# The second conformer block in the memory of the first, and the late delta-rule groups in the first priority class

## The chip, the cores and the metric

The kernel runs on one core of a Trainium2 chip. The metric is device time in microseconds (us), the median of several runs. The engines are TensorE (PE in the profile; PEld is its weight load), VectorE (DVE), ScalarE (ACT), GpSimd (POOL) and SyncE (SP, whose work here is a queue of DMA transfers). Each engine takes its own instructions strictly in the order in which the program lists them.

## The reference

One layer of a hybrid trunk over 2048 prompt tokens and 32 sample tokens, width 1024. All mixers read one normalised input; their outputs stand side by side in front of one output projection:

```python
h = rmsnorm(x, norm_mix)
z = h @ w_in                              # one projection for all three mixers
a = gated_deltanet(z, state_gdn)          # 4 heads x 128, short conv, delta rule
s = s5(z, state_s5)                       # 16 x 16 channels, complex diagonal scan
c = swish(layernorm(causal_dwconv31(glu(z), state_conv)))   # conformer, 256 wide
x = x + concat([a, s, c]) @ w_out
u = rmsnorm(x, norm_ffn)
x = x + (silu(u @ w1) * (u @ w3)) @ w2    # hidden 2816 = 22 tiles of 128
x = x + sigmoid(x @ pe_gate) * (p @ pe_w)
y = rmsnorm(x, norm_final)
```

The depthwise convolution of the conformer has 31 taps over time. The delta rule goes through the tokens in order, with a state that is handed on, so the group of tokens b waits for the group of tokens b-1.

## The kernel before, in words

The tokens are cut into four blocks of 512; the last one also carries the 32 sample tokens (544 columns, worked as 2 x 272). Activations lie transposed, features on the partitions. Every matrix product of the trunk is made in three passes of eight matmuls (high half by high half, high by low, low by high: names ending in `h` and `l`, as `fah`, `fal`, `wh_w`, `wl_w`), all at line 122 in `dense`. The low halves of the weights are made at L98, on VectorE or POOL.

The program runs in two phases. Phase A projects blocks 0 to 3 (A0 to A3; weights `wh_qkv`, `wh_z`). Phase F does the rest, block by block (F0 to F3): the output projection (`wh_out`, its operand split into `fah` and `fal` at L1134 and L1136 from tiles `hb` that a DMA brings from `mixT`, L1155), the residual (L1173), the norm (sums of squares L1167, then L154, L68 to L70), the hidden tiles j = 0 to 21, each a product with w1 (evacuated by L1196, L1199) and one with w3 (L1201, L1202, the split L1204). They go in groups of four with two tiles ahead, and then follows the product with w2 (L1218). After that come eight gate tiles (`wh_gate`, evacuated by L1242 into `gth`, L1243 into `hb`), the final norm (L1253 on VectorE) and the store (L1254). The results of the dense products share three PSUM buffers (`ps_d`).

The mixers ("heads") run beside these products. Each is a Python generator; a chain of generators is advanced one step whenever a certain number of matmul columns has been emitted (7168, in F0 9216), and each `yield` ends a step. What the steps write is:

- `conformer_block`: 31 taps for each of two halves of the channels (L824 opens, L826 sixty times, on VectorE, from `xc` and `cacc` in SBUF), then transposes (`ps_ct` L837, `ps_cf` L856), the layer norm, and the result to `mixT` (L865).
- `gdn_group`: one delta-rule group of 256 tokens, two per block, and one for the 32 sample tokens after block 3. Preparation (L909 to L947), a triangular inversion by many small steps (L982, L983), a trip through memory and `XT` (L992), the state part (`ps_vn` L1069, `ps_s` L1076, `ps_o` L1083 and L1084, on VectorE L1060, L1071, L1079), a norm (L1093 to L1101), transposes `ps_ot` (L1109), `zy` (L1110) and the DMA to `mixT` (L1111).
- the S5 units.

Block 0's mixers run during A1 to A3. After phase A, `later_heads` is one chain: conformers 1 and 2, delta rule 1, S5, delta rule 2, conformer 3, delta rule 3 with the sample group. Before each F block the chain is run until that block's mixers are complete.

The order on each engine is made when the program is built: a scheduler plays the program through on a model, and takes among the instructions that are ready the one with the lowest priority number. There are three classes, `first` (evacuations, loads, what an F block does outside its products), `heads` and `later` (the dense products and whatever the chain of heads emits). Within a class the order is that of emission. `at(which)` selects the class for what is emitted inside it. Memory also sets the order: a tile that reuses another's memory waits for that tile's last reader.

Of the kernel before, what the change touches and what calls it, by code (L numbers as in the profile page):

```python
# [1257 lines left out]
def trunk_kernel(ctx: ExitStack, tc: tile.TileContext, A):  # L1258
# [7 lines left out]
    @contextmanager  # L1266
    def at(which):
        old = getattr(G, "cur", None)
        if old is not None:
            G.pr[old] = tc.cur_priority  # L1270
        G.cur = which
        tc.cur_priority = G.pr[which]
        yield
        G.pr[which] = tc.cur_priority
        G.cur = old
        if old is not None:
            tc.cur_priority = G.pr[old]
# [33 lines left out]
    NB = G.NB  # L1311
# [60 lines left out]
    R = lambda name, bufs=1: tc.tile_pool(name=name, bufs=bufs, side="right", reuse_waits="tile")  # L1372

    def conf(b, wp):
        return conformer_block(G, A, b, wp, G.psM)

    def gdn_part(b, i, S, sp):
        S = yield from gdn_group(G, A, sp, G.psM, G.tp_, b * 4 + 2 * i, P, 2, S, b, 256 * i)
        if b == NB - 1 and i == 1:
            nc.sync.dma_start(A.gdn_p, S)  # L1380
            Sd = G.kp.tile([P, NH, P], F32, tag="S", name="Sd0")
            nc.sync.dma_start(Sd, A.st_gdn)
            Sd = yield from gdn_group(G, A, sp, G.psM, G.td_, 0, TS, 1, Sd, b, BLK)
            nc.sync.dma_start(A.gdn_s, Sd)
        return S

    state = [S]

    def conf_of(b):
        with R(f"cc_{b}") as wp:  # L1390
            yield from conf(b, wp)

    def s5_of(u):
        with R(f"s5_{u}") as wp:
            yield from s5_unit(G, A, u, wp, G.psM)

    def gdn_of(b):
        with R(f"gd_{b}", 2) as sp:
            for i in range(2):
                state[0] = yield from gdn_part(b, i, state[0], sp)  # L1400

    def run(*gens):

# [3 lines left out]
    with ExitStack() as cx:  # L1407
        pa = PhaseA(G, A, cx)
        pa.block(0)

        box = {}

        def first_s5():
            while "w5" not in box:
                yield 1
            yield from s5_unit(G, A, 0, box["w5"], G.psM)
            box["done"] = True

        def first_heads():
            with R("s5i") as tp:  # L1420
                yield from s5_init(G, A, tp, G.psM)
            with R("s5_0") as w5:
                box["w5"] = w5
                yield from conf_of(0)
                yield from gdn_of(0)
                while "done" not in box:
                    yield 1

        G.start(first_heads())
        for b in range(1, NB):  # L1430
            if b == G.UB:
                G.start(first_s5())
            pa.block(b)
        if NB == G.UB:
            G.start(first_s5())
        G.flush()
# [2 lines left out]

    def later_heads():  # L1440

        first = list(range(1, min(3, NB)))
        with ExitStack() as cx2:
            wps = [cx2.enter_context(R(f"cc_{b}")) for b in first]
            for b, wp in zip(first, wps):
                yield from conf(b, wp)
        for b in range(1, NB):
            if b not in first:
                yield from conf_of(b)
            if b % G.UB == 0:  # L1450
                yield from s5_of(b // G.UB)
            yield from gdn_of(b)
            ready[0] = b

    G.start(later_heads())
    for b in range(NB):
        G.flush(lambda: ready[0] >= b)
# [117 lines left out]
```

## Time and profile before

| | us |
|---|---|
| median of 3 runs | 2885.08 |
| lowest, highest | 2883.63, 2887.02 |
| profiled execution | 2883.21 |
| its span in the trace | 2881.4 |
| TensorE busy | 2760.5 (96%) |
| VectorE busy | 1737.5 (60%) |
| mean granted TensorE clock | 0.977 |

The page cuts the span in 40 equal slices of 72 us and gives the busy share of each engine in tenths. A row of the timeline has the start, the duration, the engine, the line, the operation with output and inputs, the count of equal operations merged in it, and in brackets the idle time ahead of it with what ended it. A row of a group has the count, the busy time and the mean in ns, then the idle time ahead.

A3 ends at 667.8 us in the trace, F1's first product is at 1228.2, F2's at 1776.3 and F3's at 2342.7.

### The profile page before, as it was taken

What the parts mean: (1) busy time and instruction counts of PE and PEld (TensorE: products, weight loads), DVE (VectorE), ACT (ScalarE), POOL (GpSimd) and SP (SyncE); (2) the same over time, 40 slices, a digit from 0 to 9 for tenths busy, and PEclk for the clock granted to TensorE, in tenths of its full rate; (3) what the DMA queues carried; (4) which work ended last, traced back from release to release, by engine and by line L of the source; (5) the groups of instructions that cost most, each with busy time, mean ns of one, the idle gap of its engine ahead of it and who ended that gap; (6) DMA issues with size and microseconds to landing.
All of it is one profiled execution on the core that took longest, in us unless ns stands there. A gap on an engine that the chain in (4) does not pass through costs nothing.

```text
span 2881.4 us, 41027 instructions
## 1 busy us (share of the span) xinstructions
PE 2760.5 (96%) x15300; PEld 2363.4 (82%) x15300; DVE 1737.5 (60%) x3933; ACT 937.7 (33%) x1409; POOL 560.0 (19%) x460
## 2 busy tenths in 40 slices
PE   7899989997999999999999999999999979999997
PEld 5668778896888888888888887788888769999997
DVE  8969765896647575665664646864663733333343
ACT  4243422323322222433423333342332423222232
POOL 4732321243333242421000101100010110000000
PEclk9999999998999999999999999999999979999998
DMA  6588776674555564686665657566565564555553
GB/s 225 169 265 262 252 229 220 202 224 166 195 184 191 167 198 162 221 270 214 213 192 171 191 165 247 190 207 193 171 195 151 193 206 155 176 175 176 176 184 105
DMA packets 278919, 565.32 MB, mean 196 GB/s; under 512 B 67344, under 2 KB 126880, under 8 KB 278576
## 3 DMA queue, kind: packets, MB, share of 16 engines
q1 hardware_dynamic: 278720, 562.70, 60.7%
q8 instruction: 121, 1.98, 0.3%
q14 instruction: 78, 0.64, 0.1%
HBM read 457.76 MB, written 104.25 MB: 195 GB/s over the span
## 4 chain that ended last, share of the span: by engine, by line
PE 78%; DVE 11%; DMA 5%; issue 2%; ACT 2%; SPq 1%; POOL 0%; DVEq 0%; ACTq 0%; POOLq 0%
PE ps_d L122 70%; DVE cacc L826 1%; PE ps_kk L935 1%; DVE gacc L625 1%; DMA sild<-gacc 1%; PE ps_q L1013 1%; PE ps_z L1026 1%; PE ps_o L1084 1%; PE ps_o L1083 1%; PE ps_s L1076 1%; DVE ct L982 0%; PE ps_ks L1056 0%; DVE cx L983 0%; PE ps_vn L1069 0%; DVE hb L1253 0%
## 5 line engine op out<-in xcount | busy, mean ns | idle before, releaser
L94 ACT ACTIVATE wh_w<-wr_w 128x1024 fp32r<-128x1024 f32 (+1 forms) x272 | 281.4, 1035 | 759.6 <-PE ps_d L122 553.5
L122 PE MATMUL ps_d<-fah,wh_w 128*128 128x512 f32 (+1 forms) x1760 | 376.8, 354 | 6.1 <-DVE hb L1173 3.5
L122 PE MATMUL ps_d<-fah,wl_w 128*128 128x512 f32 (+1 forms) x1760 | 376.5, 353 | 0.0
L122 PE MATMUL ps_d<-fal,wh_w 128*128 128x512 f32 (+1 forms) x1760 | 372.7, 352 | 0.0
L122 PEld LDWEIGHTS ps_d<-fah,wh_w 128*128 128x128 f32 x1760 | 291.2, 189 | 52.1 <-issue 4.5
L122 PEld LDWEIGHTS ps_d<-fal,wh_w 128*128 128x128 f32 x1760 | 291.3, 188 | 43.9
L122 PEld LDWEIGHTS ps_d<-fah,wl_w 128*128 128x128 f32 x1760 | 290.9, 189 | 43.1
L1218 DVE TENSOR_TENSOR hb<-hb,ps_d 128x512 f32<-128x512 f32 (+1 forms) x240 | 140.0, 585 | 192.5 <-PE ps_d L122 192.0
L122 PE MATMUL ps_d<-acth,wh_w 128*128 128x512 f32 (+1 forms) x880 | 210.4, 354 | 0.0
L122 PE MATMUL ps_d<-acth,wl_w 128*128 128x512 f32 (+1 forms) x880 | 209.9, 353 | 0.0
L122 PE MATMUL ps_d<-actl,wh_w 128*128 128x512 f32 (+1 forms) x880 | 208.7, 353 | 0.0
L826 DVE SCALAR_TENSOR_TENSOR cacc<-xc,cc_w,cacc 128x512 f32<-128x512 f32 (+1 forms) x240 | 177.9, 775 | 0.0
L122 PEld LDWEIGHTS ps_d<-actl,wh_w 128*128 128x128 f32 x880 | 149.0, 188 | 22.4
L122 PEld LDWEIGHTS ps_d<-acth,wh_w 128*128 128x128 f32 x880 | 148.2, 188 | 22.5 <-issue 0.2
L122 PEld LDWEIGHTS ps_d<-acth,wl_w 128*128 128x128 f32 x880 | 148.5, 188 | 21.8
L98 POOL TENSOR_TENSOR wl_w<-wr_w,wh_w 128x1024 fp32r<-128x1024 f32 (+1 forms) x46 | 107.6, 2339 | 254.0 <-ACT wh_w L94 228.1
L1196 DVE TENSOR_TENSOR fa<-ps_d,bc 128x512 f32<-128x512 f32 (+1 forms) x110 | 64.7, 589 | 141.2 <-PE ps_d L122 134.1
L1201 DVE SCALAR_TENSOR_TENSOR fth<-ps_d,bc 128x512 f32<-128x512 f32 (+1 forms) x110 | 64.8, 589 | 129.1 <-PE ps_d L122 128.5
L122 PE MATMUL ps_d<-hh,wh_qkv 128*128 128x512 f32 (+1 forms) x480 | 105.6, 363 | 17.0 <-DVE raw L615 15.2
L1204 DVE TENSOR_TENSOR actl<-fa,acth 128x512 fp32r<-128x512 f32 (+1 forms) x110 | 87.7, 797 | 44.3 <-ACT acth L1203 43.9
L122 PEld LDWEIGHTS ps_d<-hh,wh_qkv 128*128 128x128 f32 x480 | 81.4, 194 | 31.5 <-issue 17.0
L122 PE MATMUL ps_d<-hh,wl_qkv 128*128 128x512 f32 (+1 forms) x480 | 104.6, 359 | 2.3 <-POOL wl_qkv L98 2.3
(479 smaller groups left out, 4787.6 us busy)
## 6 DMA issues: line engine op xcount, KB each, us to landing
wr_w<-in_w SPq DMA_DIRECT2D x256, 512.0 KB, 4.3
wl_w<-lo_w SPq DMA_DIRECT2D x192, 512.0 KB, 3.7
lo_w<-wl_w SPq DMA_DIRECT2D x64, 512.0 KB, 2.9
wr_qkv<-in_w_in SPq DMA_DIRECT2D x48, 512.0 KB, 4.2
wl_qkv<-lo_qkv SPq DMA_DIRECT2D x36, 512.0 KB, 5.2
wr_out<-in_w_out SPq DMA_DIRECT2D x32, 512.0 KB, 4.8
wr_gate<-in_pe_gate SPq DMA_DIRECT2D x32, 512.0 KB, 4.1
wl_out<-lo_out SPq DMA_DIRECT2D x24, 512.0 KB, 3.5
```

The lines of the kernel that those rows point to most:

```text
L94: nc.scalar.activation(wh, wr, AF.Copy)
L98: e.tensor_tensor(wl, wr, wh.bitcast(F32), op=ALU.subtract)
L122: nc.tensor.matmul(ps[:, :cn], a[:, i, :], x(k)[:, c0:c0 + cn], start=start and p_ == 0 and i == 0, stop=stop and p_ == 2 and i == K - 1)
L625: V.scalar_tensor_tensor(acc, raw[:, t:t + W], cw[:, m, t:t + 1], acc, op0=ALU.mult, op1=ALU.add)
L826: V.scalar_tensor_tensor(acc[:, j], xc[:, j, t:t + W], cn_.w[:, j, t:t + 1], acc[:, j], op0=ALU.mult, op1=ALU.add)
L935: nc.tensor.matmul(kk4[:, h - h0], kq[:, 2 * h, cw], kq[:, 2 * h:2 * h + 2, cw], start=True, stop=True)
L1013: nc.tensor.matmul(heads3(pq, bb)[:, h], U[a, w * NH + h, bb], half(XT[a, w * NH + h], 0), start=True, stop=True)
L1026: nc.tensor.matmul(heads3(pz, a)[:, h], qs[w][bb, h, a], half(X[bb, w * NH + h], 1), start=True, stop=True)
L1196: V.tensor_tensor(a, p1[:, :cn], bc[:, cs], op=ALU.mult)
L1201: V.scalar_tensor_tensor(th, p3[:, :cn], 0.5, bc[:, cs], op0=ALU.mult, op1=ALU.mult)
L1204: V.tensor_tensor(fb[:, cs], a, fa[:, cs].bitcast(F32), op=ALU.subtract)
L1218: V.tensor_tensor(hb[m][:, c0:c0 + cn], hb[m][:, c0:c0 + cn], p_[:, :cn], op=ALU.add)
```

## The change

Two edits. First, `later_heads` opens the pool of conformer 1, runs it and closes it, and then the same with conformer 2, which so gets the memory that conformer 1 has left. Before, both pools were open at once, and both blocks could run as soon as there was an idle place. On the way only every second `yield` of conformer 1 is passed on, so that it takes ten steps of the chain fewer, and all that follows comes ten steps earlier. Second, the delta-rule groups of blocks 2 and 3 (the sample group with them) are emitted in the class `first`, where those of block 1 stay in the class of the chain.

```diff
+    def urgent(gen):
+
+        while True:
+            with at("first"):
+                try:
+                    v = next(gen)
+                except StopIteration as e:
+                    return e.value
+            yield v
+
     def gdn_of(b):
         with R(f"gd_{b}", 2) as sp:
             for i in range(2):
-                state[0] = yield from gdn_part(b, i, state[0], sp)
+                part = gdn_part(b, i, state[0], sp)
+
+                state[0] = yield from (urgent(part) if b > 1 else part)
...
     def later_heads():
 
-        first = list(range(1, min(3, NB)))
-        with ExitStack() as cx2:
-            wps = [cx2.enter_context(R(f"cc_{b}")) for b in first]
-            for b, wp in zip(first, wps):
-                yield from conf(b, wp)
+        for b in range(1, min(3, NB)):
+            for i, w in enumerate(conf_of(b)):
+                if b > 1 or i % 2:
+                    yield w
         for b in range(1, NB):
-            if b not in first:
+            if b > 2:
                 yield from conf_of(b)
```

**TensorE from A3 to F0.** Before, after the last product of A3 (`wh_z`) come the state part of block 0's second delta-rule group, the transposes of conformers 1 and 2 and the group's `ps_ot`, and then the first out-projection:

```order
L1069 MATMUL ps_vn<-rk,X 128x128 x4
L1076 MATMUL ps_s<-vn,rk 128x128 x4
...
L837 MATMUL ps_ct<-ident,cacc 128x128 x8
L1109 MATMUL ps_ot<-ident,o 128x128 x8
L856 MATMUL ps_cf_8245<-ident,ctk 128x128
...
L856 MATMUL ps_cf_8246<-ident,ctk 128x128
L122 MATMUL ps_d<-fah,wh_out 128x512 x22
```

Now:

```order
L122 MATMUL ps_d<-hh,wh_z 128x272 x8
L1109 MATMUL ps_ot<-ident,o 128x128 x4
L122 MATMUL ps_d<-hh,wl_z 128x272
L1109 MATMUL ps_ot<-ident,o 128x128 x4
...
L122 MATMUL ps_d<-hh,wl_z 128x272 x8
L122 MATMUL ps_d<-hl,wh_z 128x272 x8
L837 MATMUL ps_ct<-ident,cacc 128x128 x4
L122 MATMUL ps_d<-fah,wh_out 128x512 x12
L837 MATMUL ps_ct<-ident,cacc 128x128 x4
L122 MATMUL ps_d<-fah,wh_out 128x512 x10
```

The delta-rule group has moved in among A3's products; of the heads only four transposes of conformer 1 are left between the last product of A3 and the first of F0.

**VectorE in F0, one hidden tile.** Before, between the evacuations of F0's first hidden tiles stand pieces of block 1's delta rule, and no taps (all 120 of conformers 1 and 2 lie in A3). Now, in the middle of hidden tiles 3 and 4:

```order
L1196 TENSOR_TENSOR fa<-ps_d,bc_7367 128x512
L826 SCALAR_TENSOR_TENSOR cacc<-xc,cc_w,cacc 128x512
L98 TENSOR_TENSOR wl_w_7786<-wr_w_7783,wh_w_7785 128x1024
L826 SCALAR_TENSOR_TENSOR cacc<-xc,cc_w,cacc 128x512 x2
L1199 SCALAR_TENSOR_TENSOR fa<-fth,fa 128x512
L826 SCALAR_TENSOR_TENSOR cacc<-xc,cc_w,cacc 128x512 x2
L1201 SCALAR_TENSOR_TENSOR fth<-ps_d,bc_7367 128x512
L826 SCALAR_TENSOR_TENSOR cacc<-xc,cc_w,cacc 128x512 x2
L1202 TENSOR_TENSOR fa<-fa,fth 128x512
L826 SCALAR_TENSOR_TENSOR cacc<-xc,cc_w,cacc 128x512 x2
L1196 TENSOR_TENSOR fa<-ps_d,bc_7367 128x512
```

Conformer 2's taps, sixty in all, stand in ones, twos and threes between the steps of hidden tiles 0 to 5, and conformer 1's alone are left in A3.

**VectorE from F2 to F3.** These are the last gate evacuations of F2 and the end of the sample group. Before:

```order
L983 TENSOR_TENSOR cx<-cx,ct 16x8
L1242 SCALAR_TENSOR_TENSOR gth_20583<-gth_20583,ps_d 128x512
...
L992 STREAM_TRANSPOSE XT<-X 32x128
L1242 SCALAR_TENSOR_TENSOR gth_20628<-gth_20628,ps_d 128x512
...
L1101 TENSOR_TENSOR o<-o,or_19582 32x512
L1253 SCALAR_TENSOR_TENSOR hb<-hb,g_6863,bc_20635 128x512 x5
L1110 SCALAR_TENSOR_TENSOR zy<-ps_ot,gnw,zy 128x128
L1136 TENSOR_TENSOR fal<-hb,fah 128x544 x5
```

Now:

```order
L983 TENSOR_TENSOR cx<-cx,ct 16x8
L1242 SCALAR_TENSOR_TENSOR gth_20442<-gth_20442,ps_d 128x512
L1243 SCALAR_TENSOR_TENSOR hb<-gth_20442,hb 128x512
L992 STREAM_TRANSPOSE XT<-X 32x128
...
L1101 TENSOR_TENSOR o<-o,or_19367 32x512
L1242 SCALAR_TENSOR_TENSOR gth_20538<-gth_20538,ps_d 128x512
L1243 SCALAR_TENSOR_TENSOR hb<-gth_20538,hb 128x512
L1110 SCALAR_TENSOR_TENSOR zy<-ps_ot,gnw,zy 128x128
...
L1136 TENSOR_TENSOR fal<-hb,fah 128x544 x5
L1242 SCALAR_TENSOR_TENSOR gth_20628<-gth_20628,ps_d 128x512
```

The gate tiles are gth_20442 (the fourth), 20538 (the sixth), 20583 (the seventh) and 20628 (the eighth). The inversion now ends before the fourth evacuation instead of the seventh, `zy` stands before the seventh instead of behind the final norm, and F3's splits (`fal`) stand ahead of the eighth.

## The prediction

> **What bounds the kernel now.** I read the busy shares and the tenths, then TensorE's waits, then the two seams where TensorE thins out, by windows and row by row. First the page:
>
> ```profile
> PE 2760.5 (96%) x15300; PEld 2363.4 (82%) x15300; DVE 1737.5 (60%) x3933; ACT 937.7 (33%) x1409; POOL 560.0 (19%) x460
> PE   7899989997999999999999999999999979999997
> DVE  8969765896647575665664646864663733333343
> ```
>
> TensorE is the bound; a slice is 72 us. It drops to 7 in slice 9 (648 to 720 us, where the projections end and F0 begins) and in slice 32 (2305 to 2377 us, where F2 passes to F3). The waits over the whole span:
>
> ```profile
> engine line waited for: us in total, times, longest us
> PE ps_d L122 <- ACT fah L1134: 25.7, 5, 13.3
> ```
>
> `fah` is the rounded copy of the mixers' output, the first operand of the output projection. The seams, cut at TensorE's own starts (us, then busy time and count of each engine, granted clock, DMA share, GB/s):
>
> ```profile
> 667.79:704.80 37.01, 19.22 (x118) 15.52 (x116) 19.25 (x60) 12.06 (x22) 10.75 (x12) 0.74 0.37 122
> 704.80:714.12 9.32, 8.92 (x22) 6.12 (x23) 5.32 (x6) 4.89 (x8) 5.12 (x4) 0.59 0.96 322
> 714.12:723.79 9.67, 9.67 (x44) 7.88 (x42) 1.57 (x3) 4.22 (x5) 3.08 (x2) 1.00 0.94 308
> 1228.18:1237.00 8.82, 8.72 (x38) 6.68 (x36) 8.69 (x16) 2.00 (x4) 4.31 (x4) 1.00 1.00 385
> 1776.26:1792.23 15.97, 13.29 (x50) 10.01 (x49) 15.97 (x21) 5.15 (x8) 3.42 (x3) 0.89 0.91 318
> 2316.00:2342.74 26.74, 9.69 (x49) 6.02 (x48) 13.16 (x27) 4.64 (x7) 6.57 (x5) 0.58 0.51 177
> 2342.74:2348.89 6.15, 5.94 (x22) 5.39 (x23) 3.99 (x4) 4.54 (x7) 4.42 (x3) 0.50 1.02 371
> ```
>
> Row 3 is dense pace: 44 products in 9.67 us, 0.22 each. Rows 4 and 5 are the seams F0-F1 and F1-F2, where nothing of the mixers is late. Rows 1, 2, 6 and 7 are the two bad seams. What stands in the first of them:
>
> ```profile
> 666.79 1.16 PE L122 MATMUL ps_d<-hl,wh_z 128*128 128x272 f32 x8
> 667.79 0.60 PE L837 MATMUL ps_ct<-ident,cacc 128*128 128x128 f32 x4
> 690.19 1.97 PE L1109 MATMUL ps_ot<-ident,o 128*128 128x128 f32 x8 [1.95 <-DVE o L1101]
> 699.00 0.38 SPq L1111 DMA_DIRECT2D mixT<-zy  x1
> 701.37 3.18 SPq L1155 DMA_DIRECT2D hb<-mixT  x7
> 704.80 1.65 PE L122 MATMUL ps_d<-fah,wh_out 128*128 128x512 f32 x3 [9.15 <-ACT fah L1134]
> ```
>
> The projections end at 667.79; block 0's delta-rule group finishes only after that (its last transposes `ps_ot` at 690.19), its result goes to memory (699.00) and back (701.37), and only then does F0 start. The small products in between go at about 0.11 us (8 of 272 columns, the larger kind beside them, take 1.00 us from start to start, 666.79 to 667.79: 0.125 each).
>
> The second:
>
> ```profile
> 2306.82 0.16 DVE L983 TENSOR_TENSOR cx<-cx,ct 16x8 f32<-16x8 f32 x1
> 2309.95 0.69 DVE L1242 SCALAR_TENSOR_TENSOR gth<-gth,ps_d 128x512 f32<-128x512 f32 x1 [2.98 <-ACT gth L1241]
> 2314.97 0.30 DVE L992 STREAM_TRANSPOSE XT<-X 32x128 f32<-32x128 f32 x1 [1.91 <-DMA X<-xd]
> 2316.86 0.69 DVE L1242 SCALAR_TENSOR_TENSOR gth<-gth,ps_d 128x512 f32<-128x512 f32 x1 [1.59 <-ACT gth L1241]
> 2328.83 6.51 DVE L1253 SCALAR_TENSOR_TENSOR hb<-hb,g,bc 128x512 f32<-128x512 f32 x5
> 2335.27 0.34 DVE L1110 SCALAR_TENSOR_TENSOR zy<-ps_ot,gnw,zy 128x128 f32<-128x128 f32 x1
> 2342.74 1.78 PE L122 MATMUL ps_d<-fah,wh_out 128*128 128x272 f32 x6 [13.31 <-ACT fah L1134]
> ```
>
> The sample tokens' group ends its inversion (L983) 8 us before `XT`, and `zy`, its last step, stands behind F2's five final-norm products; TensorE waits 13.31 us.
>
> **The change, part by part.**
>
> *Seam A-F0.* A3 loses conformer 2's 60 taps and the delta-rule group moves up: its last `ps_ot` now stand in the second of the last four `wh_z` tiles, and behind the last product only four `ps_ct` come ahead of F0. Excess now: rows 1 and 2 last 46.33 us; dense they would take 118 x 0.11 = 13.0 and 22 x 0.22 = 4.8: 28.5 us. What remains is bounded by the good seams: F0-F1 8.82 - 38 x 0.22 = 0.5, F1-F2 15.97 - 50 x 0.22 = 5.0. I take 2.5, between the two, as nothing but conformer work follows. **Gain 26** (20 to 28, the lower end if the write to memory and back costs the 5.8 us of 699.00 to 704.80 again). Moved past on SyncE's queue: the eight `hb` loads, now ahead of the last `zgd` writes.
>
> *Seam F2-F3.* The chain is ten steps shorter, and its inversion ends before the fourth gate evacuation instead of the seventh; gates come 6.91 us apart (2309.95, 2316.86), so about 21 us earlier. `zy` gets ahead of the final norm, and the first out-projection follows the last gate pass. Excess now: 32.89 - 49 x 0.11 - 22 x 0.125 = 24.7. F3's `fah` lies in the buffers that the last gate pass reads, so something stays, as at F1-F2: 5.0. **Gain 20** (14, if the eighth gate evacuation waits for the five `fal` now ahead of it; 24).
>
> *Conformer 2's taps in F0.* They no longer cost in A3; they are 60 operations more on VectorE, between F0's normalisation and hidden 5, nine or ten a hidden, ahead of evacuations that free PSUM. The rows (the first two of A3, the others of F0):
>
> ```profile
> L826 DVE SCALAR_TENSOR_TENSOR cacc<-xc,cc_w,cacc 128x512 f32<-128x512 f32 x120 | 85.8, 753 | 0.0
> L824 DVE TENSOR_SCALAR cacc<-xc,cc_w,cc_b 128x512 f32<-128x512 f32 x4 | 2.1, 532 | 0.7 <-DMA xc<-xcd 0.7
> L1204 DVE TENSOR_TENSOR actl<-fa,acth 128x512 fp32r<-128x512 f32 x22 | 35.4, 1607 | 10.2 <-ACT acth L1203 10.2
> L98 DVE TENSOR_TENSOR wl_w<-wr_w,wh_w 128x1024 fp32r<-128x1024 f32 x22 | 27.8, 1265 | 7.1 <-ACT wh_w L94 7.0
> L1199 DVE SCALAR_TENSOR_TENSOR fa<-fth,fa 128x512 f32<-128x512 f32 x22 | 20.9, 949 | 3.3 <-ACT fth L1198 3.3
> L1202 DVE TENSOR_TENSOR fa<-fa,fth 128x512 f32<-128x512 f32 x22 | 20.8, 945 | 0.5
> L1201 DVE SCALAR_TENSOR_TENSOR fth<-ps_d,bc 128x512 f32<-128x512 f32 x22 | 15.2, 689 | 30.0 <-PE ps_d L122 29.8
> L1196 DVE TENSOR_TENSOR fa<-ps_d,bc 128x512 f32<-128x512 f32 x22 | 15.1, 687 | 19.8 <-PE ps_d L122 16.5 <-ACT bc L135 3.2
> L98 POOL TENSOR_TENSOR wl_w<-wr_w,wh_w 128x1024 fp32r<-128x1024 f32 x42 | 102.0, 2429 | 241.8 <-ACT wh_w L94 216.0 <-DMA zy<-zgd 11.6 <-DVE cx L983 8.6
> 754.04 0.70 PE L122 MATMUL ps_d<-fah,wh_w 128*128 128x512 f32 x2
> 764.41 0.16 DVE L68 TENSOR_TENSOR rst<-rsy 128x4 f32<-128x4 f32 x1 [1.14 <-POOL rsy L67]
> 763.25:840.00 76.75, 76.75 (x337) 62.71 (x336) 43.77 (x60) 22.43 (x27) 24.38 (x12) 1.00 0.52 178
> ```
>
> The last row is F0's pace: 76.75 us for 337 products, 0.228 each, so 5.47 us for the 24 of one half of a hidden tile (w1 or w3). VectorE starts 10 us behind TensorE (764.41 against 754.04). Up to the sixth tile's last PSUM release it has 57 taps (0.753) and two openings (0.532): 44.0; five splits (1.265): 6.3; and 28 steps of hidden tiles, 6 x 4.88 less the last two (2.55): 26.7. That is 10 + 77 = 87 us. TensorE, which has a PSUM buffer in hand, would be 13 halves on, 71 us. Loss 16 by the means. If each of the 28 steps took the 0.69 of the two evacuations (19.3 instead of 26.7), about 8; if on this short sum each of the six weight splits on POOL (2.43) also held VectorE up, 14.6 more, about 23. I take **14**: the means of these rows come from all of F0, with stretches in which the delta rule works on POOL as well.
>
> Why a step can be long is seen here:
>
> ```profile
> 782.06 2.41 POOL L98 TENSOR_TENSOR wl_w<-wr_w,wh_w 128x1024 fp32r<-128x1024 f32 x1 [5.43 <-DVE fth L1201]
> 782.78 2.23 DVE L1202 TENSOR_TENSOR fa<-fa,fth 128x512 f32<-128x512 f32 x1
> ```
>
> The DVE step is 0.68 elsewhere; here it ends within 0.6 us of POOL's. The Trainium skill ("SBUF — State Buffer", Who interferes with whom) says that a VectorE instruction with two SBUF inputs and a GpSimd instruction that reads SBUF exclude each other, the second waiting for the whole of the first. It speaks against this change, since a tap has two such inputs. By that rule, strictly, the loss would be near 23, without it near 8; the row means lie between.
>
> *The class of blocks 2 and 3's groups.* The order on VectorE within F1 and F2 is nearly the one of before; where a piece now precedes an evacuation (0.2 to 0.7 us), three PSUM buffers cover it: 1 (0 to 3). *Conformer 3 at F1-F2:* its taps begin 20 VectorE instructions earlier relative to the seam; the same work stands before the same waits: 0 (-3.5 to +3.5, the `hb` wait below). *Memory:* conformer 2's load waits for conformer 1's last tap; SyncE has it in F0 behind weight loads, long after: 0.
>
> ```profile
> PE ps_d L122 <- DVE hb L1173: 3.5, 1, 3.5
> ```
>
> *Sum:* -26 - 20 + 14 + 1 = -31. The profiled execution is 2883.2 us (span 2881.4 and 1.8 around it), 1.9 under the median of 2885.1, so 2852 by its scale, **2854** by that of the median.
>
> **The rivals.**
> *Only the first seam closes:* the sample group is still late, since from `XT` it needs a DMA, TensorE, ScalarE and two trips through memory, 27.8 us from 2314.97 to 2342.74. For: 1.91 us of waiting on a DMA. Against: 6.5 of the 27.8 are the norm, and 21 us are won. Time 2854 + 20 = **2874**.
> *The taps cost nothing:* VectorE is idle 43% of the time in F0 (43.77 of 76.75 us busy), 33 us there, and the 44 us of taps would fit under some 100 us. Against: the order puts them into six tiles, 66 us. Time 2854 - 14, with 1 left over from the start: **2841**.
>
> *Slower:* in F0 VectorE, not TensorE, sets the pace and each tap is fully on the path, at more than the 0.855 of the wider taps through POOL's splits. It decides from 46 / 60 = 0.77 us a tap. At 0.855 the 60 cost 51, against 46 gained: with the 1 and some for POOL, **2892**.
> *Nothing comes of it:* each seam closes by half only, because the wait returns at the next operand (an `hb` load, a `zgd` write ahead of it on SyncE), and the taps cost their high end: -23 + 23, 2885.
>
> **How the numbers follow.** Forecast 0.68; only one seam 0.13; no tap cost 0.08; slower 0.06; nothing 0.05. The forecast's own ends, each against its taken value (below 2, 4, 6, 1, 3.5; above 6, 6, 9, 2, 3.5), make 8 below and 13 above as the root of their squares: 2846 to 2867. To take in the untaxed case at 2841 and the one-seam case at 2874, with 5 and 2 us to spare, the range is 2836 to 2876; slower, nothing and the tails stay outside. 0.2% is 5.8 us, about what three runs can tell from no change: faster 0.89, same 0.05, slower 0.06.
>
> **What would show it.** Right: TensorE's tenth for 648 to 720 us is 9, and its wait for `fah` is near 5 us in all; in F0's first six hidden tiles VectorE has no idle time, and TensorE waits some 14 us for `fa` (L1196) and `fth` (L1201); `zy` (L1110) ahead of L1253 at the last seam. Wrong: a wait of over 5 us for `fah` at either seam, or for `fa` of over 30 us.

## The result, and the profile after

| | before | after |
|---|---|---|
| median, us | 2883.63 (5 runs, 2880.08 to 2887.02) | 2859.95 (5 runs, 2856.63 to 2862.68) |
| ratio | | 0.9917, 95% interval 0.9905 to 0.9929 |
| profiled execution, us | 2883.21 | 2862.39 |
| span | 2881.4 | 2860.6 |

The change makes the kernel 23.7 us faster. The forecast was 2854, which is 31 us under the median of the first three runs (2885.08). The page's rows of busy time and of TensorE's and VectorE's tenths, after:

```profile
PE 2756.9 (96%) x15300; PEld 2357.1 (82%) x15300; DVE 1747.6 (61%) x3933; ACT 934.4 (33%) x1409; POOL 558.0 (20%) x460
PE   8789999999899999999999999999999999999997
DVE  8969764865877466576564646865663743333343
```

The 7 of slice 32 is gone and the 7 of slice 9 is a 9 (slices counted from 0, as in the prediction). In their place one new 8 stands behind the projections, in slice 10 (715 to 787 us), and VectorE has an 8, 7, 7 from just there on.

Cut at the first product of A3 (`wh_qkv`), and at the first out-projection of F0, F1, F2 and F3, the windows of before (time, TensorE busy and count, weight load, VectorE, ScalarE, POOL, granted clock, DMA):

```profile
560.33:704.80 144.47, 124.90 (x978) 119.69 (x976) 123.45 (x273) 35.64 (x62) 54.05 (x60) 0.93 0.57 187
704.80:1228.18 523.38, 521.30 (x2480) 428.52 (x2481) 324.22 (x554) 165.93 (x233) 181.58 (x87) 0.99 0.58 193
1228.18:1776.26 548.08, 545.55 (x2669) 450.10 (x2668) 311.61 (x750) 189.68 (x277) 56.87 (x44) 0.99 0.65 203
1776.26:2342.74 566.48, 539.56 (x2577) 440.31 (x2575) 352.95 (x840) 191.03 (x291) 52.92 (x41) 0.97 0.60 191
```

and of after:

```profile
561.31:682.46 121.15, 118.94 (x951) 117.21 (x949) 77.90 (x179) 26.00 (x44) 33.12 (x49) 0.97 0.60 189
682.46:1242.93 560.47, 534.74 (x2512) 436.84 (x2509) 374.71 (x653) 172.84 (x249) 198.34 (x99) 0.97 0.57 191
1242.93:1789.58 546.65, 543.64 (x2670) 446.87 (x2668) 331.78 (x767) 190.81 (x279) 56.08 (x43) 1.00 0.64 203
1789.58:2322.66 533.08, 530.44 (x2566) 432.93 (x2564) 329.88 (x806) 190.49 (x291) 48.00 (x38) 1.00 0.61 193
```

A3 is 23.3 us shorter, F2 with its seam to F3 33.4 us, and **F0 is 37.1 us longer**; F1 is 1.4 shorter, and what lies outside these windows adds 0.3. TensorE's idle time (first number less second) goes from 19.6 to 2.2 in A3, from 2.1 to 25.7 in F0, and from 26.9 to 2.6 in F2. The rest of F0's growth, 13.4 us, is busy time: 27 products that A3 no longer has now stand behind it (F0 has 32 more), and the clock of F0 is lower (0.97 for 0.99).

The seam A-F0 in TensorE's timeline after:

```profile
681.10 1.16 PE L122 MATMUL ps_d<-hl,wh_z 128*128 128x272 f32 x8
682.10 0.60 PE L837 MATMUL ps_ct<-ident,cacc 128*128 128x128 f32 x4
682.46 0.70 PE L122 MATMUL ps_d<-fah,wh_out 128*128 128x512 f32 x2
683.84 1.41 PE L122 MATMUL ps_d<-fah,wh_out 128*128 128x512 f32 x4 [0.68 <-ACT fah L1134]
```

Four transposes lie between the phases, and the wait for `fah`, 9.15 us before, is 0.68. The seam F2-F3, VectorE and TensorE:

```profile
2286.28 0.15 DVE L983 TENSOR_TENSOR cx<-cx,ct 16x8 f32<-16x8 f32 x1
2292.94 0.30 DVE L992 STREAM_TRANSPOSE XT<-X 32x128 f32<-32x128 f32 x1 [1.29 <-DMA X<-xd]
2310.45 0.34 DVE L1110 SCALAR_TENSOR_TENSOR zy<-ps_ot,gnw,zy 128x128 f32<-128x128 f32 x1
2320.82 2.00 PE L122 MATMUL ps_d<-fal,wh_gate 128*128 128x512 f32 x8
2322.66 1.13 PE L122 MATMUL ps_d<-fah,wh_out 128*128 128x272 f32 x7
```

The sample group's `zy` is done 12 us before the last gate pass ends, and the out-projection follows that pass with no gap. Now F0's waits after:

```profile
PE ps_d L122 <- DVE fth L1201: 6.9, 1, 6.9
PE ps_d L122 <- DVE fa L1196: 5.7, 1, 5.7
PE ps_q L1013 <- DVE XT L992: 4.3, 2, 3.3
PE ps_y L526 <- DMA c_Toep<-s5Toep: 3.8, 1, 3.8
PE ps_bc L134 <- DVE rso L70: 2.3, 1, 2.3
```

The first, second and fifth are one VectorE that is behind: two stalls, 8.0 and 6.9 us, 14.9 together. The other two have nothing to do with taps: `XT` belongs to block 1's delta rule, `c_Toep` is a load of the S5 unit. Where the two stalls begin and end, in the timelines:

```profile
746.18 1.00 DVE L824 TENSOR_SCALAR cacc<-xc,cc_w,cc_b 128x512 f32<-128x512 f32 x2 [2.36 <-DMA xc<-xcd]
748.23 2.38 DVE L69 SCALAR_TENSOR_TENSOR rst<-rms_v,rst 128x4 f32<-128x4 f32 x1
751.86 0.15 DVE L70 SCALAR_TENSOR_TENSOR rso<-rst,rsy 128x4 f32<-128x4 f32 x1
752.15 0.62 PE L134 MATMUL ps_bc<-ident,rso 128*128 128x128 f32 x4 [2.33 <-DVE rso L70]
758.43 3.41 PE L122 MATMUL ps_d<-fah,wh_w 128*128 128x512 f32 x8 [5.66 <-DVE fa L1196]
811.80 5.17 POOL L98 TENSOR_TENSOR wl_w<-wr_w,wh_w 128x1024 fp32r<-128x1024 f32 x2 [6.70 <-ACT wh_w L94]
811.96 2.80 DVE L826 SCALAR_TENSOR_TENSOR cacc<-xc,cc_w,cacc 128x512 f32<-128x512 f32 x1
814.68 2.84 DVE L1204 TENSOR_TENSOR actl<-fa,acth 128x512 fp32r<-128x512 f32 x1
822.18 2.04 PE L122 MATMUL ps_d<-acth,wh_w 128*128 128x512 f32 x4 [6.95 <-DVE fth L1201]
```

At the first, the load of conformer 2's `xc` holds VectorE 2.36 us at the head of its queue, with F0's norm (L69, L70) behind it. The memory itself had long been free, since conformer 1's last tap began at 615.60; the load is issued only at 740.28, at the place in SyncE's queue that the scheduler gave it. L69, a 128x4 operation, takes 2.38 us beside a POOL split. At the second, two splits on POOL hold a tap and an L1204 for 2.8 us each, where each takes 0.7 elsewhere.

### The profile page after: what moved, and what is told of

It is laid out like the page before. It is cut to its first block, busy times and chain, and to the rows that moved or that the text cites. A ratio compares the mean times of both kernels' runs of the same rounds, so it can differ in the third digit from the quotient of the medians.

```text
span 2860.6 us, 41024 instructions
## 1 busy us (share of the span) xinstructions
PE 2756.9 (96%) x15300; PEld 2357.1 (82%) x15300; DVE 1747.6 (61%) x3933; ACT 934.4 (33%) x1409; POOL 558.0 (20%) x460
## 4 chain that ended last, share of the span: by engine, by line
PE 66%; DVE 17%; DMA 9%; issue 3%; SPq 2%; ACT 2%; POOL 1%; DVEq 0%; ACTq 0%; POOLq 0%
PE ps_d L122 58%; DVE cacc L826 4%; DVE gacc L625 1%; DMA xk<-in_xT 1%; PE ps_q L1013 1%; DMA cu<-ud 1%; PE ps_z L1026 1%; DVE ct L982 1%; DMA sild<-gacc 1%; DMA hb<-mixT 1%; PE ps_kk L935 1%; DVE cx L983 1%; DMA xc<-xcd 1%; PE ps_ks L1056 1%; PE ps_o L1083 1%
## 5 line engine op out<-in xcount | busy, mean ns | idle before, releaser
L122 PE MATMUL ps_d<-fal,wh_w 128*128 128x512 f32 (+1 forms) x1760 | 378.9, 354 | 0.0
L1218 DVE TENSOR_TENSOR hb<-hb,ps_d 128x512 f32<-128x512 f32 (+1 forms) x240 | 140.0, 584 | 182.1 <-PE ps_d L122 181.1
L826 DVE SCALAR_TENSOR_TENSOR cacc<-xc,cc_w,cacc 128x512 f32<-128x512 f32 (+1 forms) x240 | 186.3, 807 | 0.0
L98 POOL TENSOR_TENSOR wl_w<-wr_w,wh_w 128x1024 fp32r<-128x1024 f32 (+1 forms) x46 | 114.8, 2496 | 276.5 <-ACT wh_w L94 246.3
L1203 ACT ACTIVATE acth<-fa 128x512 fp32r<-128x512 f32 (+1 forms) x110 | 60.2, 547 | 163.7 <-DVE fa L1202 163.7
L1204 DVE TENSOR_TENSOR actl<-fa,acth 128x512 fp32r<-128x512 f32 (+1 forms) x110 | 81.3, 739 | 46.8 <-ACT acth L1203 46.5
```

Of the source, the lines that this page charges most:

```text
L98: e.tensor_tensor(wl, wr, wh.bitcast(F32), op=ALU.subtract)
L122: nc.tensor.matmul(ps[:, :cn], a[:, i, :], x(k)[:, c0:c0 + cn], start=start and p_ == 0 and i == 0, stop=stop and p_ == 2 and i == K - 1)
L826: V.scalar_tensor_tensor(acc[:, j], xc[:, j, t:t + W], cn_.w[:, j, t:t + 1], acc[:, j], op0=ALU.mult, op1=ALU.add)
L1203: nc.scalar.activation(fa[:, cs], a, AF.Copy)
L1204: V.tensor_tensor(fb[:, cs], a, fa[:, cs].bitcast(F32), op=ALU.subtract)
L1218: V.tensor_tensor(hb[m][:, c0:c0 + cn], hb[m][:, c0:c0 + cn], p_[:, :cn], op=ALU.add)
```

## The experiments

Each ratio is against runs of the kernel before on the same chip. The last three columns are of one profiled execution each: length of the stretch from F0's first out-projection to F1's (F0), TensorE's idle time in it, and the stretch F2 to F3. Executions of one kernel differ by up to 8 us either way, so between two kernels the intervals count, and the columns say where a difference lies. The scheduler makes a new order for every kernel, so an edit can also move work that it does not name.

| kernel | median, us | ratio, interval | F0 | idle | F2 |
|---|---|---|---|---|---|
| before, on the three chips used | 2879.57 to 2884.38 | 1 | 523.4 | 2.1 | 566.5 |
| after | 2859.95 | 0.9917 (0.9905 to 0.9929) | 560.5 | 25.7 | 533.1 |
| e1 memory and steps only | 2886.08 | 1.0014 (1.0005 to 1.0024) | 558.8 | 25.2 | 561.4 |
| e2 class only | 2864.53 | 0.9939 (0.9922 to 0.9955) | 523.4 | 2.5 | 550.1 |
| e4 class and steps | 2856.75 | 0.9919 (0.9901 to 0.9938) | 547.8 | 11.5 | 529.2 |
| e8 class and memory | 2881.40 | 0.9990 (0.9978 to 1.0003) | 541.5 | 14.0 | 568.1 |
| e3 after without the 60 taps | 2848.15 | 0.9883 (0.9868 to 0.9897) | 547.3 | 12.9 | 533.1 |
| e5 after, 7 splits to VectorE | 2845.46 | 0.9868 (0.9849 to 0.9887) | 548.4 | 15.1 | 533.1 |
| z1 after, 22 splits to VectorE | 2841.38 | 0.9869 (0.9854 to 0.9885) | 539.4 | 12.1 | 533.2 |
| z2 after, 6 splits to POOL | 2856.74 | 0.9932 (0.9913 to 0.9951) | 559.3 | 26.9 | 533.1 |
| z3 e5 with early `xc` | 2842.79 | 0.9873 (0.9854 to 0.9891) | 546.6 | 13.7 | 534.7 |
| z4 before, 7 splits to VectorE | 2881.42 | 1.0006 (0.9996 to 1.0017) | 522.3 | 1.6 | 566.8 |
| e12 conformer 3 early | 2909.25 | 1.0092 (1.0070 to 1.0114) | 522.4 | 2.9 | 532.3 |
| e13 conformers 2 and 3 moved | 2946.95 | 1.0223 (1.0201 to 1.0245) | 520.8 | 2.2 | 530.3 |

**e1: memory and steps only.**

```diff
-                state[0] = yield from (urgent(part) if b > 1 else part)
+                state[0] = yield from part
```

> The first half of the change alone: conformer 2 in conformer 1's memory and the ten steps fewer, the delta-rule groups all in the old class. Theory (memory buys the seam A-F0 and pays more in F0; the class buys F2-F3): -22 at A-F0, +37 in F0, nothing to -8 later, so 2890 to 2899, slower than before. Rival (the ten steps alone bring the sample group forward, the class does little): F2-F3 closes too, 2866 or less. In the order the sample group ends its inversion before the seventh gate evacuation, as before.

Slower than before, as the theory had it, but by 0.14% and not by 7 us or more: A3 is 117.3 us long, 27 less than before, and F0 takes it all and more (558.8, 35.5 longer than before). F0's waits are those of the whole change (`fth` 6.7, `fa` 5.7, `XT` 4.4, `c_Toep` 3.6, `rso` 2.0), so the class has no part in them. F2 gains 5.1 us. So the ten steps alone do not bring the sample group forward.

**e2: class only.**

```diff
-        for b in range(1, min(3, NB)):
-            for i, w in enumerate(conf_of(b)):
-                if b > 1 or i % 2:
-                    yield w
+        first = list(range(1, min(3, NB)))
+        with ExitStack() as cx2:
+            wps = [cx2.enter_context(R(f"cc_{b}")) for b in first]
+            for b, wp in zip(first, wps):
+                yield from conf(b, wp)
```

> The second half alone: groups of blocks 2 and 3 in the class of the evacuations, later_heads as before. Theory: A-F0 keeps its 22 us, F0 has no taps and no stall, F2-F3 gains 20 to 27: 2857 to 2864, as fast as the whole change. Rival (class does little without the ten steps): 2875 to 2884.

The median, 2864.53, lies 0.5 above the theory's range. F0 is the one of before to 0.1 us, and F2 is 16.4 us shorter, half of the whole change's 33.4. By the ratios, most of what the kernel gained (0.61 of 0.83%) comes with this half of the change alone.

**e4: class and steps, both pools open.**

```diff
+        first = list(range(1, min(3, NB)))
+        with ExitStack() as cx2:
+            wps = [cx2.enter_context(R(f"cc_{b}")) for b in first]
+            for b, wp in zip(first, wps):
+                for i, w in enumerate(conf(b, wp)):
+                    if b > 1 or i % 2:
+                        yield w
```

> The whole change without the shared memory: both conformer pools open as before, conformer 1 at half the steps, the late groups in the first class. Theory (the taps in F0 are what costs 37 us, and the seam A-F0 is worth 22): no tap in F0, 2850 to 2857, faster than the change. Rival (the ten steps earlier chain crowds F0, whatever the taps): 37 stays without the 22, 2880 to 2890.

The total fits the theory, and its reason does not: F0 has no tap, and is 24.4 us longer than before all the same. The rival had named this, with too large a size (37). The windows of F0 and F2 (the profiled execution, 2865.28 us, is the slowest of its four runs and 8.5 above their median, so some of its length may be its own):

```profile
703.47:1251.26 547.79, 536.32 (x2557) 439.73 (x2558) 342.78 (x624) 166.15 (x236) 186.19 (x92) 0.98 0.57 192
1796.22:2325.42 529.20, 528.51 (x2566) 433.62 (x2564) 321.05 (x792) 190.07 (x291) 47.60 (x38) 1.00 0.61 197
```

Idle is 11.5 us in F0 (waits for L983, `XT`, L1218, `c_Toep`), and 77 more products stand in it than before (2557 for 2480), while F1 has 75 fewer (2594 for 2669): part of F0's length is work that came forward, not loss. Against e2 the steps cost F0 24.4, and give 1.8 in F1 and 20.9 in F2.

**e3: the change without conformer 2's taps.** The convolution of block 2 is left out but for its opening product.

```diff
+                if b != 2:
                 V.scalar_tensor_tensor(acc[:, j], xc[:, j, t:t + W], ...
```

> The change, with conformer 2's sixty taps left out (its convolution is the opening product only; everything after them stays). Theory: F0 loses its stalls, the slow clock after them and the later waits, 34 to 37 us less than the change: 2823 to 2827. Rival (only the two stalls that the trace names for the taps, 15 us, come from them): 2845. Rival (steps): 2855 to 2860.

11.8 us less than the change by the medians, 10 by the ratios: far from the theory's 34, between the two rivals and nearest to the first, that only the two stalls come from the taps. F0 is 547.3 us: 13.1 below the change and still 24.0 above before:

```profile
678.25:1225.59 547.34, 534.47 (x2558) 436.82 (x2558) 349.85 (x627) 174.30 (x252) 198.87 (x102) 0.99 0.59 199
```

With e4, that is two kernels without a tap in F0 that both keep some 24 us of its growth. As in e4 a part of it is work that came forward: F0 has 78 products more than before, and F1 47 fewer (2622 for 2669).

**e8: the steps undone.**

```diff
-            for i, w in enumerate(conf_of(b)):
-                if b > 1 or i % 2:
-                    yield w
+            yield from conf_of(b)
```

> The change with every yield of conformer 1 passed on, so that the chain keeps its old pace; shared memory and first class stay. Theory (of F0's 37 us the taps are some 13, and the chain that runs ten steps ahead is the rest, by delta-rule and S5 pieces that come before their operands): TensorE idle in F0 falls from 25.7 to about 15 us and F0 lasts about 548 us (523 before, 560 in the change). Its order has the sample group behind the final norm again, so F2-F3 stays open and the whole is 2868 to 2880. Rival (all of F0's loss is the taps): F0 stays at 557 to 562 us, idle 24 to 27.

F0's idle is 14.0 us, where the theory had 15, and F0 541.5, shorter than the 548 expected; the median is 1.4 above its range. F0's window and its waits:

```profile
678.82:1220.32 541.50, 527.49 (x2490) 431.89 (x2490) 378.72 (x637) 172.07 (x248) 192.84 (x95) 0.98 0.56 189
PE ps_d L122 <- DVE fth L1201: 6.4, 1, 6.4
PE ps_d L122 <- DVE ct L982: 2.9, 1, 2.9
PE ps_q L1013 <- DVE XT L992: 1.4, 1, 1.4
PE ps_d L122 <- DVE fa L1196: 1.0, 2, 0.7
```

So undoing the steps takes 19.0 us off F0's 37.1 (560.5 - 541.5), and 18.1 stay with the taps at the old pace. Of the two stalls of the change only the second is left (`fth` 6.4). The wait for `rso` is gone and that for `fa` is 1.0, so the first stall needs the steps as well as the taps. `XT` falls from 4.3 to 1.4 and `c_Toep` is no longer among the waits. Taps and steps do not simply add: e3, with the steps and without the taps, keeps 24.0, and 24.0 + 18.1 is 5 more than 37.1.

F2 stays as long as before, in the same class `first`: in the shared memory class and steps each need the other at the last seam (566.5 before, 561.4 and 568.1 with one of the two, 533.1 with both). With two pools the class alone had shortened F2 to 550.1 (e2); why the shared memory takes that away is open.

**e5, z1, z2, z4: where the weight splits are made.** e5 and z1 change one line, z2 and z4 likewise:

```diff
-            e = nc.vector if name == "w3" else nc.gpsimd
+            e = nc.vector if name == "w3" or (name == "w1" and key < 7) else nc.gpsimd   # e5, z4
+            e = nc.vector if name in ("w1", "w3") else nc.gpsimd                          # z1
+            e = nc.vector if name == "w3" and key > 5 else nc.gpsimd                      # z2
```

> The change, with the low halves of w1 for hidden tiles 0 to 6 of F0 made on VectorE instead of POOL (seven splits of 128x1024). Theory (a POOL split holds up one VectorE step for about 2 us, a VectorE split takes 1.2): TensorE's two long waits in F0 fall from 15 to about 9 us and the whole to about 2854. Rival (VectorE just has too much to do, POOL does not matter): seven splits more at 1.2 are 8.5 us more, 2868.

> The change with all 22 w1 splits of F0 on VectorE, where the kernel with seven moved gave 2845. Theory (a POOL split matters only where VectorE sets the pace, which is beside the taps): nothing more to win behind hidden tile 6, 2843 to 2849. Rival (every POOL split costs): fifteen more at 0.9 us, 2832.

> The change with the splits the other way: w3 of hidden tiles 0 to 5 on POOL too, so that VectorE has six splits of 1.2 us less to do and POOL six of 2.4 more. Theory of exclusion (each POOL split holds a VectorE step for some 2 us): 6 x (2.0 - 1.2) = 5 us slower than the change, 2865. Rival (VectorE's own load is what counts): 6 x 1.2 = 7 us faster, 2853.

> The kernel before, with w1's splits of hidden tiles 0 to 6 on VectorE. Theory (the splits matter only beside the taps): no difference, 2880 to 2887. Rival (POOL splits cost by themselves): as much as in the changed kernel, 14 us faster, 2869.

e5 gives VectorE seven splits more, in the stretch where it is the bound, and the kernel gets **faster** than the change; the intervals of the two ratios lie apart. The second stall goes from 6.9 us to 0.8, the first from 8.0 to 5.9 (`rso` 3.4 and `fa` 2.5):

```profile
PE ps_d L122 <- DVE fa L1196: 2.5, 1, 2.5
PE ps_d L122 <- DVE fth L1201: 0.8, 1, 0.8
```

The gain, some 14 us, is larger than the theory's 6. The stalls give 8.2 of it; the waits for `XT` and `c_Toep` are also 5.0 shorter (2.3 and 0.8), which the theory does not explain. That POOL's splits are what holds the taps shows within e5: POOL makes no split between 744 and 797 us, and the taps there take 0.76 us or less; each of the next three splits holds one tap to about 2.8. The second of these three:

```profile
803.02 2.41 POOL L98 TENSOR_TENSOR wl_w<-wr_w,wh_w 128x1024 fp32r<-128x1024 f32 x1 [3.56 <-ACT wh_w L94]
803.12 2.86 DVE L826 SCALAR_TENSOR_TENSOR cacc<-xc,cc_w,cacc 128x512 f32<-128x512 f32 x1
```

In z4, without taps in F0, the same line does nothing, as expected. z1's median is 2 us under its theory's range, but its ratio is e5's, so fifteen splits more bring nothing that can be told. z2 goes the other way: its median tells nothing (its interval overlaps that of the change), but the taps' mean does: 905 and 1051 ns. The taps' group in VectorE's rows, over 115 us from 45 us after F0's first product on, in the change and then in z2:

```profile
L826 DVE SCALAR_TENSOR_TENSOR cacc<-xc,cc_w,cacc 128x512 f32<-128x512 f32 x60 | 52.1, 905 | 0.0
```

```profile
L826 DVE SCALAR_TENSOR_TENSOR cacc<-xc,cc_w,cacc 128x512 f32<-128x512 f32 x60 | 60.4, 1051 | 0.0
```

Six POOL splits more make the sixty taps 8.3 us longer, more than the six VectorE splits that they replace (6 x 1.2). In e5 the same row has 858 ns. TensorE's waits in F0 for the norm, the evacuations and the last tap grow with it, from 14.9 us to 20.2 in z2 (`rso` 1.0 and these three):

```profile
PE ps_d L122 <- DVE fa L1196: 10.1, 2, 7.9
PE ps_ct L837 <- DVE cacc L826: 6.7, 1, 6.7
PE ps_d L122 <- DVE fth L1201: 2.4, 3, 0.9
```

The waits for `XT` and `c_Toep` are shorter (2.2 and 1.0), so F0's idle time is about that of the change. POOL's splits pay too: 3074 ns of mean in the change, 2459 in e5.

**z3: conformer 2's input in memory of its own.** e5, and:

```diff
+        with R("xc_2") as xp:
+            for b in range(1, min(3, NB)):
+                with R(f"cc_{b}") as wp:
+                    for i, w in enumerate(conformer_block(G, A, b, wp, G.psM, xp if b == 2 else None)):
```

> The kernel with seven w1 splits moved to VectorE, and conformer 2's input xc in memory of its own, so that its load need not wait for conformer 1's last tap. Eight taps then stand ahead of F0's norm on VectorE, where it was idle. Theory (2.4 us of the first stall are the wait for that load): the wait for rso and fa at F0's first hidden tile falls from 5.9 to 3 us or less, 2840 to 2844. Rival (the taps between the norm's steps set it, wherever the load is): 2845 to 2849.

The median lies in the theory's range, but the ratio is e5's, and the stall is not shorter (rso 4.0, fa 2.5 against 3.4 and 2.5): the load is issued before 558.1 us and no longer waited for, and the taps between the norm's steps take its place. The rival holds.

**e12 and e13: conformer 3 (and 2) elsewhere.** In e12, on top of e2, conformer 3 is emitted ahead of block 2's S5 and delta rule; in e13 conformer 2 too comes only behind block 1's delta rule, with empty steps in its old place:

```diff
+            if b == 2:
+                for w in conf_of(2):     # e13 only
+                    pass
+                yield from conf_of(3)
```

> Conformers 1 and 2 as before the change (two pools, all steps), the late groups in the first class, and conformer 3 emitted ahead of S5 and the delta rule of block 2, not behind it. Theory (the sample group is late because its group's memory is that of conformer 3, whose taps stand at F1-F2; the ten steps brought those taps forward): F2-F3 closes wholly, F0 stays clean, 2850 to 2857. Rival (taps cost the same wherever they stand, here in F0's gate tiles and F1's out-projection): 2862 to 2868.

> Both seams at once: conformer 1 alone ahead of delta rule 1 (eighteen empty steps stand where conformer 2's were), conformer 2 and then conformer 3 behind delta rule 1, late groups in the first class. Theory: A-F0 gains 23 and F2-F3 33, F0's hidden tiles have no taps and the chain its old pace; the taps in F1's first hidden tiles find no weight splits beside them and cost 0 to 8: 2826 to 2836. Rival (sixty taps cost 13 us wherever they stand): 2840 to 2853.

Both missed by far, and not in the stretches that they were made for: F0 is 522.4 and 520.8, F2 532.3 and 530.3, within 3 or so of the shortest here. It is F1 that grows, to 613 and 675 us:

```profile
1229.26:1842.27 613.01, 563.05 (x2721) 462.96 (x2719) 377.35 (x865) 202.21 (x303) 72.96 (x56) 0.95 0.60 193
```

```profile
PE ps_q L1013 <- DVE XT L992: 30.4, 1, 30.4
PE ps_ot L1109 <- DVE o L1101: 16.8, 2, 10.2
PE ps_nrm L907 <- ACT qsq L904: 10.4, 1, 10.4
```

The window is e12's F1 (50 us idle), the waits are e13's in F1 (30 us for one `XT`): now it is block 2's delta rule that comes too late. That its memory lies behind conformer 3's taps, as the sample group's did, follows from the order of the pools and was not tried apart.

**The best version** is e5 (or z1 or z3, which the intervals do not tell from it): 1.3% under before, 0.5% under the change.

## Why the prediction came out right, point by point

- *Seam A-F0*, forecast 26, measured 23.3. The reading of the order was right, and so was the bound: what remains are waits of 1.6 us and less. Of the 23.3, 17.4 are idle time; the other 6.0 are busy time, 27 products that moved to F0 and a higher clock (0.93 to 0.97).
- *Seam F2-F3*, forecast 20, measured 33.4 over F2. The step was under-sized. The idle time of F2 falls by 24.3, near the 24.7 of the sum, but nothing stays where I had left 5.0; F1-F2's wait for `hb` (3.5) went to about 1, where I had put 0; and 9.1 are busy time, which the sum priced at nothing: the clock of F2 rises from 0.97 to 1.00, and it has 11 products fewer.
- *Taps in F0*, forecast 14, measured 14.9 for the two stalls, and 13.1 (e3) to 18.1 (e8) in the length of F0. This term was right in its size, and in its cause as far as VectorE goes: it has no idle time between 748 and 826 us, and both stalls end on `rso`, `fa` and `fth`. That the first stall is all but gone without the ten steps (e8) was not foreseen. The rule of the Trainium skill ("SBUF — State Buffer", Who interferes with whom) that the forecast weighed is what the trace shows, with e5's taps beside and without POOL's splits, and its sign is shown by e5, z2 and z4: beside two-input VectorE work a POOL split holds a step for about 2.1 us (2.80 against 0.73), a split on VectorE itself takes 1.2. It was not strictly once per split, so the loss came out near the means' 16 and not at 23.
- *Mis-sized: the class and the steps*, forecast 1. The 1 us rests on three PSUM buffers covering a piece that now precedes an evacuation. I read that from the order within F1 and F2, where it holds (F1 is 1.4 shorter); the sum has no term for what the ten steps do to F0. There block 1's delta rule and S5 come earlier, and TensorE meets them before their operands: 4.3 us for `XT`, 3.8 for `c_Toep`. The steps make 19.0 (e8) to 24.0 us (e3) of F0. Beyond these waits and the first stall that is work that came forward from F1 and F2, and the clock; no run splits it further.
- So errors of opposite sign, 13 too little gain at F2 against 22 too little loss in F0 and 3 too much gain in A3, leave 10 us between the sum and the profiled execution (2852 and 2862.4), and 6 between the medians (2854 and 2859.95). That the median came so near is luck: the errors offset each other, and with F0's error alone it would have been at the upper end of the range, 2876. The one-seam rival and the untaxed one are out by the windows. So is the slower one: 13.1 to 18.1 us for sixty taps are 0.2 to 0.3 us a tap, where it needed 0.77. What e1 does show is that the first half of the change alone does not pay.
- The signs that were named: the tenth for the seam is 9, VectorE has no idle time beside the taps, `zy` is ahead of the final norm, and TensorE waits 12.6 us for `fa` and `fth` in the two stalls (some 14 forecast). Its wait for `fah` is 1.6 us in all, less than the 5 expected.

## What to carry to other kernels

A change that closes a gap between stages by moving work into the next stage is priced by the engine that gets the work, in the stretch where it gets it: sixty VectorE taps of 0.73 us are 44 us of work, which F0's idle time on VectorE (38% of 523 us before) would hold several times over, and yet they cost 13 to 18 us where they stand between evacuations. When an order is made by a scheduler, moving one chain forward moves all its successors, so every seam behind it has to be read, not only the one that was meant (e12 cleared F2 and lost 65 us in F1). Where VectorE with two SBUF inputs is the bound, as beside the taps here, taking POOL's work onto it can be the faster choice (e5), and moving more to POOL was no relief (z2).

## What the runs showed of the hardware

The price of a TensorE stall is more than its length. After the wait of 5.66 us the first eight products took 3.41 us (row 758.43), where eight take 2.00 elsewhere, and after 6.95 us four took 2.04 for 1.09 and the next four 1.91. That is 1.4 and 1.8 us on top of the waits. The granted clock in 24 us around each:

```profile
755.95:779.95 24.00, 21.52 (x88) 17.51 (x89) 24.00 (x34) 6.10 (x8) 5.22 (x2) 0.89 0.31 109
803.95:827.95 24.00, 17.05 (x68) 13.44 (x68) 23.15 (x29) 5.31 (x8) 8.63 (x4) 0.86 0.50 171
```

By the clock it is at most 24 x 0.11 = 2.6 and 24 x 0.14 = 3.4 us, an upper bound, since each window also holds a part of the wait itself. And a 128x4 operation on VectorE can take 2.38 us (L69) when it meets a POOL split, where it takes 0.16 in e5 without one, and that is nearly as long as a large one: the hold does not go by the size of the step that is held.
